# Regrouping the five far head pairs of a dilated attention layer: 2, 2, 1 in place of 1, 2, 2

## The chip, the core and the metric

The kernel runs on one core of a Trainium2 chip. The metric is the device time of one execution in microseconds (us). The core has five engines that are used here: TensorE (PE in the profile, with its weight loads as PEld), VectorE (DVE), ScalarE (ACT), GpSimd (POOL) and SyncE (SP, which here only starts transfers). They run side by side and wait for each other through semaphores. Each works through its own list of instructions in the order in which they stand there.

## The reference

A decoder trunk of two residual layers over 512 tokens of width 1024, all float32. The first layer mixes tokens by causal pooling, the second by attention; each is followed by a SwiGLU of inner width 2816, and one norm ends it. What matters here is the attention of the second layer. Its 16 heads of width 64 form three groups: heads 0 to 5 look at near keys (window 128, dilation 1), heads 6 to 10 at keys 4 apart, heads 11 to 15 at keys 16 apart.

```python
def attn_mixer(h, w_qkv, w_out):
    qkv = jnp.einsum('bsd,de->bse', h, w_qkv).reshape(B, S, 3, N_HEADS, HEAD_DIM)
    q = rope(qkv[:, :, 0]) * HEAD_DIM ** -0.5
    k = rope(qkv[:, :, 1])
    v = qkv[:, :, 2]
    for (window, dilation), n_g in zip(((128, 1), (512, 4), (2048, 16)), (6, 5, 5)):
        o_g, lse_g = dilated_window_attention(q[:, :, sl], k[:, :, sl], v[:, :, sl], window, dilation)
        outs.append(o_g)
        lses.append(logsumexp(lse_g, axis=-1) - math.log(n_g))
    alpha = softmax(stack(lses, axis=-1), axis=-1)
    merged = concatenate([o_g * 3 * alpha[:, :, g] for g, o_g in enumerate(outs)], axis=2)
    return merged @ w_out
```

Inside `dilated_window_attention` each query has a masked softmax over its keys (maximum, exponential, sum), the weights multiply the values, and the log of the sum plus the maximum goes into `lse`.

## The kernel before, in words

**Products.** Each float32 product is made of three matmuls: an operand is split into a rounded high part and a rest, and high x high, high x low and low x high are added up in PSUM. So each weight tile that a DMA brings (`wraw`) goes through a cast on ACT (`whi`, line 139) and a subtraction on DVE (`wlo`, line 143). Five such tiles are held; as `weights` is called for one step, the casts of tiles for later steps are issued, and a cast can start when PE is through with the tile whose place it takes.

**Steps.** The attention is a list of numbered steps. Steps 0 to 15 are the projections of q and k for the eight head pairs t = 0 to 7 (step 2t is q of pair t, 2t + 1 is k; `project`, lines 227 to 229, 24 matmuls). After each, `rope` turns the result: DVE shuffles and multiplies (859, 860), POOL multiplies the shuffled copy (861), DVE adds (865). Steps 16 to 18 project the values of the six near heads (m = 0, 1, 2). ACT copies each result out of PSUM (`ropea`, 1115 before, 1114 after); when the next projection is issued, `turn` transposes it with four PE transposes (1106 before, 1105 after), and ACT copies them into `v` (1107, then 1106). Steps 19 to 26 project the values of the far heads, in two halves of four steps, each step with six matmuls into each of four PSUM banks (1129 to 1131, then 1128 to 1130); the results are copied out after steps 22 and 26 by ACT (1137) and DVE (1135).

**Scores.** `later(step)`, called at the end of every step, does what is due: first transposes, then at most one visit with scores. A visit falls due three steps after its last k. The near pairs t = 0, 1, 2 have a visit each (`near_scores`). The far pairs t = 3 to 7 go through `far_scores`, which takes one pair or two: PE makes eight small matmuls per pair (925; the trace shows each as two), DVE scales and masks each head into `e` (935), takes the maxima (938, 879), and ACT makes four exponentials per head (`soften`, 881). Two steps later PE transposes the first pair's weights (955, four per far head), three steps later the second's; ACT or DVE copies them into `pT` (960, 958).

**PSUM.** There are eight banks: four named `mm`, two named `sc` (pool `psc`) and two named `tp` (pool `ptr`). Each name is a ring, and a tile can be written when the last reader of the tile that had the bank is done. A visit's first pair takes the two `sc` banks, a second pair takes two `mm` banks. `turn` takes a `tp` bank for m = 0 and an `sc` bank for m = 1 and 2.

**Group weights.** After step 19 `group_sums` (1027 to 1037) combines maxima and sums over the heads: one exponential on ACT (1029), a few small DVE operations and four small DMAs. After step 21 `group_weights` (1042 to 1069) makes the groups' shares with a second exchange by DMA (1062, waited for in 1069), and after step 23 one PE transpose (1077) spreads them.

**What sets the order.** PE's instructions stand in the order of the code. The other engines' lists are ordered by a planner when the kernel is built, by dependencies and priorities, so that an edit in the code can move their instructions in ways that it does not spell out.

Of the kernel before, what the change touches and what calls it, by code (L numbers as in the profile page):

```python
# [10 lines left out]
F32 = mybir.dt.float32  # L11
# [6 lines left out]
P = 128  # L18
# [40 lines left out]
def trunk_kernel(ctx: ExitStack, tc: tile.TileContext, x_in, xT, gam, gains, consts, ident_d, w0, wT, w1, wv, w_down, out):  # L59
# [171 lines left out]
    def project(j, hi, lo):  # L231
        ps = mm.tile([P, S], F32, name="mm")
        whi, wlo = weights(j)
        for k in range(NC):
            mm3(ps, whi[:, k, :], wlo[:, k, :], hi[:, k, :], lo[:, k, :], k == 0, k == NC - 1)
        return ps
# [26 lines left out]
    class Norm:  # L263
# [49 lines left out]
        def turn(self, b, half, tp):  # L313

            for j in range(4):
                at = half * S + j * P
                nc.tensor.transpose(tp[:, j, :], self.tile(b)[:, at : at + P], ident)
# [78 lines left out]
    with ExitStack() as pctx:  # L396
# [26 lines left out]
        for c in range(NC):  # L423
# [13 lines left out]
            k = 0 if c < 2 else c % 2  # L437
# [393 lines left out]
    with ExitStack() as actx:  # L831
# [4 lines left out]
        psc = actx.enter_context(tc.tile_pool(name="psc", bufs=2, space=bass.MemoryType.PSUM))  # L836
        ptr = actx.enter_context(tc.tile_pool(name="ptr", bufs=2, space=bass.MemoryType.PSUM))
# [18 lines left out]
        def rope(ps, t, name):  # L856
            a = aw.tile([P, S], F32, name="ropea")
            sw = aw.tile([P, S], F32, name="ropeb")
            nc.vector.stream_shuffle(sw, ps, PARTNER)
            nc.vector.tensor_mul(a, ps, cosr)  # L860
            nc.gpsimd.tensor_mul(sw, sw, sinr)
            out = aw.tile([P, S], F32, name=name, bufs=3)

            if t >= 3:
                nc.vector.tensor_add(out, a, sw)
            elif name == "k":
                nc.vector.tensor_add(out.rearrange("p (b r i) -> p b r i", b=4, r=R), blocks_of(a), blocks_of(sw))
            else:
                by_r = lambda z: z.rearrange("p (r j) -> p r j", r=R)
                nc.vector.tensor_add(out.rearrange("p (j r) -> p r j", r=R), by_r(a), by_r(sw))  # L870
            return out
# [90 lines left out]
        pend_sc, pend_tr = [], []  # L962

        def later(step):


            while pend_tr and pend_tr[0][0] <= step:
                _, h, e = pend_tr.pop(0)
                transposes(h, e)
                if HEAD_GROUP[h] == 0:  # L970
                    break
            if pend_sc and pend_sc[0][0] <= step:
                _, run, args = pend_sc.pop(0)

                pend_tr.extend((step + 2 + n // 2, *got) for n, got in enumerate(run(*args)))
# [25 lines left out]
        for t in range(8):  # L1001
            pq = pqk[2 * t] if t < 2 else project(j_qk[2 * t], h_hi, h_lo)
            q = rope(pq, t, "q")
            later(2 * t)
            pk = pqk[1] if t == 0 else project(j_qk[2 * t + 1], h_hi, h_lo)
            k = rope(pk, t, "k")
            later(2 * t + 1)
            if t in (4, 6):
                first = (t, q, k)
            elif t in (5, 7):  # L1010
                pend_sc.append((2 * t + 3, far_scores, (first, (t, q, k))))
            else:
                pend_sc.append((2 * t + 3, far_scores, ((t, q, k),)) if t == 3 else (2 * t + 3, near_scores, (t, q, k)))

        ring = [ap.tile([P, S], F32, name=f"LB{g}") for g in range(3)]
        sums = ap.tile([P, 2, 3, 4], F32, name="gsums")
# [83 lines left out]

        def turn():
            m, vt = to_turn.pop(0)

            tp = ptr.tile([P, 4, P], F32, name="tp") if m == 0 else psc.tile([P, 4, P], F32, name="sc")
            for b in range(4):
                nc.tensor.transpose(tp[:, b, :], vt[:, b * P : (b + 1) * P], ident)
            nc.scalar.copy(v[:, :, m * P : (m + 1) * P], tp)

        step = 16
        for m in range(3):  # L1110
            ps = project(j_v0[m], h_hi, h_lo)
            if to_turn:
                turn()
            vt = aw.tile([P, S], F32, name="ropea")
            nc.scalar.copy(vt.rearrange("p (b r i) -> p b r i", b=4, r=R), blocks_of(ps))
            to_turn.append((m, vt))
            between(step)
            step += 1
        for part in range(2):
            at = VA + part * VB  # L1120
            pv = [mm.tile([P, S], F32, name="mm") for _ in range(4)]
            for c in range(4):
                whi, wlo = weights(j_v[part][c])
                for b in range(4):
                    for kk in range(2):
                        kc = 2 * c + kk
                        o = pv[b][:, :VB]
                        xh, xl = (z[:, kc, b * P : (b + 1) * P] for z in (h_hi, h_lo))
                        nc.tensor.matmul(o, lhsT=xh, rhs=whi[:, kk, :], start=kc == 0, stop=False)  # L1129
                        nc.tensor.matmul(o, lhsT=xh, rhs=wlo[:, kk, :], start=False, stop=False)  # L1130
                        nc.tensor.matmul(o, lhsT=xl, rhs=whi[:, kk, :], start=False, stop=kc == NC - 1)
                    if c == 3:
                        with tc.high_priority(URGENT):
                            if b // 2:
                                nc.vector.tensor_copy(v[:, b, at : at + VB], pv[b][:, :VB])
                            else:
                                nc.scalar.copy(v[:, b, at : at + VB], pv[b][:, :VB])
                if to_turn:
                    turn()
                between(step)  # L1140
                step += 1
# [105 lines left out]
```

## Time and profile before

| | |
|---|---|
| median of three runs | 1001.42 us (1000.78 to 1001.96) |
| the profiled execution | 1000.55 us |
| its span, first to last instruction | 998.8 us |
| TensorE clock granted | 0.999 of full speed |
| PE busy | 990.8 us (99%) |
| DVE busy | 784.4 us (79%) |
| ACT busy | 529.1 us (53%) |
| POOL busy | 113.1 us (11%) |
| steps 8 to 26 of the attention | about 506 to 603 us of the span |

All times inside the span are from one profiled execution; what lies outside the span (1000.55 - 998.8, about 1.8 us) is the start and the end of the launch. Rows of the timeline give the start, the duration and the engine of an instruction. Matmuls overlap, so the distance between two starts on PE tells what one costs, and the duration doesn't. Rows of the chain of waits give the start of a piece, its length, and its engine, and are read downwards in time.

### The profile page before, as it was taken

The page shows a single profiled execution, that of the slowest core. Times are in us where ns is not written, and L with a number is a line of the kernel's source. Part 1 is how long each engine was busy: PE and PEld are TensorE (multiplying, and loading weights), DVE is VectorE, ACT ScalarE, POOL GpSimd, SP SyncE. Part 2 cuts the span into 40 slices and gives each one's busy share as a digit, 9 for nine tenths or more (in the row PEclk, how much of TensorE's full clock was granted, in tenths as well). Part 3 has the DMA queues.
Part 4 walks back from the last instruction along what each step waited for, and adds up shares of the span by engine and source line. Part 5 has one row for each costly group of instructions (what it writes and reads, how often), then busy time and mean ns, then how long its engine had stood idle before and what let it go on. Part 6 is the DMA issues. An engine that isn't in the chain of part 4 may idle for free.

```text
span 998.8 us, 16590 instructions
## 1 busy us (share of the span) xinstructions
PE 990.8 (99%) x6575; PEld 908.1 (91%) x6575; DVE 784.4 (79%) x1116; ACT 529.1 (53%) x838; POOL 113.1 (11%) x114
## 2 busy tenths in 40 slices
PE   9999999999999999999999999999999999999997
PEld 8888999989989998989888899899998998999896
DVE  6475899898888888777887457479989889788875
ACT  5573666545644554573543544356654554455354
POOL 0002010110111100002112023101011101211000
PEclk9999999999999999999999999999999999999999
DMA  9457276668559755524211249527666855975522
GB/s 335 177 168 190 63 197 174 152 189 234 149 128 290 179 137 155 182 71 134 85 56 53 83 141 267 103 61 191 179 159 198 235 148 121 294 176 141 153 66 84
DMA packets 76461, 157.29 MB, mean 157 GB/s; under 512 B 5904, under 2 KB 6288, under 8 KB 76384
## 3 DMA queue, kind: packets, MB, share of 16 engines
q1 hardware_dynamic: 58000, 121.00, 36.2%
q0 software_dynamic: 18096, 34.98, 20.5%
q8 instruction: 51, 0.84, 0.3%
q10 hardware_dynamic: 288, 0.27, 0.1%
q14 instruction: 26, 0.21, 0.1%
HBM read 154.08 MB, written 2.13 MB: 156 GB/s over the span
## 4 chain that ended last, share of the span: by engine, by line
PE 98%; ACT 1%; DVE 0%; issue 0%; ACTq 0%
PE p L625 25%; PE r L625 13%; PE r L712 10%; PE mm L625 6%; PE p L712 5%; PE mm L766 4%; PE mm L227 4%; PE mm L229 4%; PE mm L228 4%; PE mm L712 2%; PE early L443 2%; PE mm L363 2%; PE mm L361 2%; PE mm L362 2%; PE mm L1129 1%; PE tp L955 1%
## 5 line engine op out<-in xcount | busy, mean ns | idle before, releaser
L139 ACT CAST whi<-wraw 128x1024 fp32r<-128x1024 f32 (+2 forms) x189 | 184.8, 981 | 184.3 <-issue 50.8
L143 DVE TENSOR_TENSOR wlo<-wraw,whi 128x1024 fp32r<-128x1024 f32 (+2 forms) x190 | 221.1, 1165 | 74.8 <-ACT whi L139 74.1
L139 ACT CAST whi<-vraw 128x1024 fp32r<-128x1024 f32 (+1 forms) x102 | 99.6, 976 | 144.8 <-DVE vraw L145 53.7
L625 PE MATMUL p<-t_hi,wlo 128*128 128x256 f32 x528 | 149.8, 284 | 0.0
L625 PE MATMUL p<-t_lo,whi 128*128 128x256 f32 x528 | 149.4, 283 | 0.0
L625 PE MATMUL p<-t_hi,whi 128*128 128x256 f32 x528 | 148.4, 281 | 0.0
L143 DVE TENSOR_TENSOR wlo<-vraw,whi 128x1024 fp32r<-128x1024 f32 (+1 forms) x102 | 114.9, 1127 | 13.9 <-ACT whi L139 13.7
L625 PEld LDWEIGHTS p<-t_hi,whi 128*128 128x128 f32 x528 | 100.0, 189 | 0.0
L625 PE MATMUL r<-h_hi,wlo 128*128 128x256 f32 x352 | 99.9, 284 | 0.0
L625 PEld LDWEIGHTS p<-t_hi,wlo 128*128 128x128 f32 x528 | 99.6, 189 | 0.0
L625 PE MATMUL r<-h_lo,whi 128*128 128x256 f32 x352 | 99.6, 283 | 0.0
L625 PEld LDWEIGHTS p<-t_lo,whi 128*128 128x128 f32 x528 | 99.3, 188 | 0.0
L625 PE MATMUL r<-h_hi,whi 128*128 128x256 f32 x352 | 99.0, 281 | 0.0
L145 DVE TENSOR_TENSOR vraw<-vraw,wraw 128x1024 f32<-128x1024 f32 x68 | 76.6, 1127 | 0.8
L107 POOL DMA_DIRECT2D wraw<-w x22 | 26.6, 1211 | 436.1 <-DVE wlo L143 126.2
L625 PEld LDWEIGHTS r<-h_hi,whi 128*128 128x128 f32 x352 | 66.7, 189 | 0.0
L625 PEld LDWEIGHTS r<-h_hi,wlo 128*128 128x128 f32 x352 | 66.4, 189 | 0.0
L625 PEld LDWEIGHTS r<-h_lo,whi 128*128 128x128 f32 x352 | 66.2, 188 | 0.0
L227 PE MATMUL mm<-h_hi,whi 128*128 128x512 f32 (+1 forms) x176 | 64.9, 369 | 0.0
L229 PE MATMUL mm<-h_hi,wlo 128*128 128x512 f32 (+1 forms) x176 | 63.6, 361 | 0.0
L228 PE MATMUL mm<-h_lo,whi 128*128 128x512 f32 (+1 forms) x176 | 63.4, 360 | 0.0
L712 PE MATMUL r<-whi,u_lo 128*128 128x512 f32 x144 | 56.1, 390 | 0.0
(329 smaller groups left out, 2493.2 us busy)
## 6 DMA issues: line engine op xcount, KB each, us to landing
wraw<-w SPq DMA_DIRECT2D x116, 512.0 KB, 4.9
wraw<-w_down SPq DMA_DIRECT2D x32, 512.0 KB, 3.6
vraw<-w SPq DMA_DIRECT2D x22, 512.0 KB, 5.5
wraw<-w POOLq DMA_DIRECT2D x22, 512.0 KB, 7.6
vraw<-w POOLq DMA_DIRECT2D x22, 512.0 KB, 9.0
wraw<-wT SPq DMA_DIRECT2D x16, 512.0 KB, 4.4
wraw<-w_down SPq DMA_DIRECT2D x24, 256.0 KB, 2.6
vraw<-w_down SPq DMA_DIRECT2D x6, 512.0 KB, 5.4
```

The source lines that it names most:

```text
L107: nc.gpsimd.dma_start(dst, more, accum_op=ALU.add)
L139: nc.scalar.copy(hi[:, :n], raw[:, :n])
L143: nc.vector.tensor_sub(lo[:, :n], raw[:, :n], hi[:, :n].bitcast(F32))
L145: nc.vector.tensor_add(raws[into][:, :n], raws[into][:, :n], raws[more][:, :n])
L227: nc.tensor.matmul(ps, lhsT=whi, rhs=xhi, start=first, stop=False, **kw)
L228: nc.tensor.matmul(ps, lhsT=whi, rhs=xlo, start=False, stop=False, **kw)
L229: nc.tensor.matmul(ps, lhsT=wlo, rhs=xhi, start=False, stop=last, **kw)
L361: nc.tensor.matmul(ps, lhsT=xhi, rhs=w[0][:, k, :], start=first, stop=False)
L362: nc.tensor.matmul(ps, lhsT=xhi, rhs=w[1][:, k, :], start=False, stop=False)
L625: nc.tensor.matmul(ps[:, g, :], lhsT=w[:, g, c, :], rhs=xx[:, c, :], start=i in (0, 1, 3) and g + c + k == 0, stop=c == 3 and k == 2, skip ...
L712: nc.tensor.matmul(acc[t], lhsT=u, rhs=w, start=i in (0, 1, 3) and c + k == 0, stop=c == len(pairs) - 1 and k == 2, skip_group_check=True,)
L766: nc.tensor.matmul(ps, lhsT=u, rhs=w[:, m, :], start=z + m + k == 0, stop=z == 1 and m == 1 and k == 2,)
```

## The change

Two edits, both in how the work is grouped; no product is added or left out.

```diff
-            if t in (4, 6):
+            if t in (3, 5):
                 first = (t, q, k)
-            elif t in (5, 7):
+            elif t in (4, 6):
                 pend_sc.append((2 * t + 3, far_scores, (first, (t, q, k))))
             else:
-                pend_sc.append((2 * t + 3, far_scores, ((t, q, k),)) if t == 3 else (2 * t + 3, near_scores, (t, q, k)))
+                pend_sc.append((2 * t + 3, far_scores, ((t, q, k),)) if t == 7 else (2 * t + 3, near_scores, (t, q, k)))
...
         def turn():
             m, vt = to_turn.pop(0)
-
-            tp = ptr.tile([P, 4, P], F32, name="tp") if m == 0 else psc.tile([P, 4, P], F32, name="sc")
+            tp = psc.tile([P, 4, P], F32, name="sc")
```

The visits with far scores were at the ends of steps 9 (pair 3), 13 (pairs 4, 5) and 17 (pairs 6, 7). They are now at the ends of steps 11 (pairs 3, 4), 15 (pairs 5, 6) and 17 (pair 7). The far transposes, eight for a pair, were at steps 11, 15, 16, 19 and 20; they are now at 13, 14, 17, 18 and 19. All three turns now take an `sc` bank, so the `sc` ring is shared between the turn at step 17 and the scores that follow at once. From line 1103 on the lines stand one lower.

The first place is PE's list at the end of step 17, behind the projection of m = 1. `sc` is a bank of that ring, `tp` one of the other, `ropea` the copied values of m = 0, `e` the exponentials of a far head. The names in brackets are the engines whose semaphores an instruction waits for. Before:

```order
L1106 MATMUL tp<-ident,ropea 128x128 [waits Activation_49]
L1106 MATMUL tp<-ident,ropea 128x128 x3
L925 MATMUL sc<-k,q 128x128 x8
L925 MATMUL mm<-k,q 128x128 [waits DVE_49]
L925 MATMUL mm<-k,q 128x128 x7
```

The same place now:

```order
L1105 MATMUL sc<-ident,ropea 128x128 [waits DVE_49,Activation_49]
L1105 MATMUL sc<-ident,ropea 128x128 x3
L955 MATMUL tp<-ident,e 128x128 x4
L955 MATMUL tp<-ident,e 128x128 [waits DVE_49]
L955 MATMUL tp<-ident,e 128x128 x3
L925 MATMUL sc<-k,q 128x128 [waits PE_49]
L925 MATMUL sc<-k,q 128x128 [waits Activation_49]
L925 MATMUL sc<-k,q 128x128 x6
```

Eight transposes now stand between the turn and the scores, one pair of scores is gone from the visit, and the second matmul of the scores waits for ACT: it writes the `sc` bank that ACT copies the turn out of.

The second place is ACT's list from the first values (m = 0) to the exponential of the group sums. Before, with the 16 exponentials of pairs 6 and 7 in the middle, here as their first and their last rows:

```order
L139 CAST whi<-wraw 128x640 [waits DMAHW5_49,PE_49,Activation_49]
L1115 COPY ropea<-mm 128x512 [waits DVE_49,PE_49]
L960 COPY pT<-tp 128x512 [waits PE_49]
L139 CAST whi<-wraw 128x640 [waits DMAHW6_49,PE_49,Activation_49]
L1115 COPY ropea<-mm 128x512 [waits DVE_49,PE_49]
L1107 COPY v<-tp 128x4x128 [waits PE_49]
L881 ACTIVATE e,den<-e,neg 128x128 [waits DVE_49]
L881 ACTIVATE e,den<-e,neg 128x128 x3
```

and now, from the last exponentials of pairs 5 and 6, which are the visit of step 15:

```order
L881 ACTIVATE e,den<-e,neg 128x128 x3
L1114 COPY ropea<-mm 128x512 [waits PE_49]
L139 CAST whi<-wraw 128x640 [waits DMAHW5_49,Activation_49]
L139 CAST whi<-wraw 128x640 [waits DMAHW6_49,PE_49,Activation_49]
L1114 COPY ropea<-mm 128x512 [waits PE_49]
L1106 COPY v<-sc 128x4x128 [waits PE_49]
L960 COPY pT<-tp 128x512 [waits PE_49]
L881 ACTIVATE e,den<-e,neg 128x128 [waits DVE_49]
```

The copy of the values of m = 0 now stands behind 16 exponentials, and two casts stand between it and the copies of m = 1 and of the turn; behind them are 8 exponentials in place of 16.

The third place is DVE's list at the end of step 15, where the visit of pairs 5 and 6 has come in:

```order
L859 STREAM_SHUFFLE ropeb<-mm 128x512 [waits PE_49]
L860 TENSOR_TENSOR ropea<-mm,angles 128x512
L143 TENSOR_TENSOR wlo<-wraw,whi 128x640 [waits DMAHW4_49,Activation_49]
L865 TENSOR_TENSOR k<-ropea,ropeb 128x512 [waits DVE_49,Pool_49]
L935 SCALAR_TENSOR_TENSOR e<-sc,gain 128x512 [waits PE_49] x2
L938 TENSOR_REDUCE mx<-e 128x4 [waits DVE_49] x2
L879 TENSOR_SCALAR neg<-mx 128x4 [waits DVE_49]
```

The scores' first DVE operation (935) stands behind the whole rope of k of pair 7 and one weight subtraction, as it stood at step 13 before behind the rope of pair 6 and a subtraction of 1024 columns.

## The prediction, before the changed kernel had run

> **What bounds the kernel now.** I read the page first, then PE's waits, then the chain of waits through the attention, then the timelines of PE, DVE and ACT around its weak places.
>
> ```profile
> span 998.8 us, 16590 instructions
> PE 990.8 (99%) x6575; PEld 908.1 (91%) x6575; DVE 784.4 (79%) x1116; ACT 529.1 (53%) x838; POOL 113.1 (11%) x114
> PE mm L261 <- DVE odd_rows L255: 1.1, 1, 1.1
> PE mm L1129 <- ACT ropea L1115: 0.3, 1, 0.3
> ```
>
> The first two rows are the page's, the other two are all of PE's waits. PE is the bound: 990.8 of 998.8 us, and it waits twice in the whole program, once at the start, which the change doesn't touch, and once for 0.3 us at step 19, for the copy of the values of m = 2. So there is little to win, and a loss needs a wait on PE that is not there now. The question is one of tenths of a microsecond: which small stalls go, and which come. The chain of waits shows what is behind the one at step 19:
>
> ```profile
> 567.70 4.78 ACT e L881 x25
> 572.64 1.34 ACT e L881 x7
> 573.98 0.47 ACT v L1107
> 574.45 0.49 ACT ropea L1115
> 574.99 0.41 PE mm L1129
> ```
>
> The visit of step 17 has four heads. Their 16 exponentials (with the reads of their sums) hold ACT from 567.70 to 573.98, and behind them stand two copies; the second frees the last `mm` bank that step 19 needs. PE's timeline shows what that costs:
>
> ```profile
> 574.42 0.31 PE L1131 MATMUL mm<-whi,h_lo 128*128 128x320 f32 x1
> 574.99 0.41 PE L1129 MATMUL mm<-whi,h_hi 128*128 128x320 f32 x1 [0.26 <-ACT ropea L1115]
> 575.24 0.31 PE L1130 MATMUL mm<-wlo,h_hi 128*128 128x320 f32 x1
> ```
>
> and a second, smaller stall of the same kind four steps later, which the list of waits doesn't name:
>
> ```profile
> 590.18 0.31 PE L1130 MATMUL mm<-wlo,h_hi 128*128 128x320 f32 x1
> 590.33 0.31 PE L1131 MATMUL mm<-whi,h_lo 128*128 128x320 f32 x1
> 590.65 0.42 PE L1129 MATMUL mm<-whi,h_hi 128*128 128x320 f32 x1
> 590.90 0.31 PE L1130 MATMUL mm<-wlo,h_hi 128*128 128x320 f32 x1
> ```
>
> These matmuls follow each other at 0.15 (590.18 to 590.33). From 574.42 to 575.24 are 0.82 where 0.30 would do: the stall costs 0.52, more than the 0.26 that the wait shows, since a matmul's record outlasts the start of the next by 0.16, and the first after a gap takes 0.1 more. From 590.33 to 590.90 are 0.57 where 0.30 would do: 0.27. The cause of the second is on DVE:
>
> ```profile
> 589.26 0.18 DVE L1069 TENSOR_TENSOR den<-den,mx 128x24 f32<-128x24 f32 x1 [3.41 <-DMA mx<-gw]
> 589.37 0.83 DVE L143 TENSOR_TENSOR wlo<-wraw,whi 128x640 fp32r<-128x640 f32 x1
> 590.11 0.88 DVE L1135 COPY v<-mm 128x320 f32<-128x320 f32 x2
> ```
>
> DVE's list stands still for 3.41 us for the second exchange of the group weights, and the copy that frees the bank (1135) comes only behind it; the first of the two ends at about 590.6.
>
> **The change part by part.** *The new wait: the turn and the scores in one ring.* At the end of step 17 PE turns m = 0 into one `sc` bank, makes eight transposes, and its second score matmul needs that bank back, once ACT has copied it. The pieces are in the trace, though not in this order:
>
> ```profile
> 563.40 0.60 PE L1106 MATMUL tp<-ident,ropea 128*128 128x128 f32 x4
> 563.92 1.16 PE L925 MATMUL sc<-k,q 64*128 64x128 f32 x16
> ...
> 576.41 1.04 PE L955 MATMUL tp<-ident,e 128*128 128x128 f32 x8
> 577.20 0.39 PE L1129 MATMUL mm<-whi,h_hi 128*128 128x320 f32 x1
> 577.43 0.31 PE L1130 MATMUL mm<-wlo,h_hi 128*128 128x320 f32 x1
> ```
>
> These are PE's. On ACT, at the same end of step 17:
>
> ```profile
> 563.41 0.73 ACT L139 CAST whi<-wraw 128x640 fp32r<-128x640 f32 x1 [4.65 <-issue]
> 564.04 0.58 ACT L1115 COPY ropea<-mm 128x512 f32<-128x512 f32 x1
> 564.52 0.59 ACT L1107 COPY v<-tp 128x512 f32<-128x512 f32 x1
> ```
>
> Call T the start of the turn (563.40 here). PE needs 0.52 for the turn, 0.79 for the transposes and about 0.13 for the first score matmul: it wants the bank at T + 1.44. ACT makes the cast that the end of step 17 released, at T, then the copy of m = 1, then the copy of the turn, which ends at 565.11, T + 1.71, and reaches PE 0.05 later (574.94 to 574.99 in the chain above). So even if ACT is free at T, PE waits 0.32: the lower end of this cost. Queued behind that matmul are the rest of the scores and the whole of step 18, so a wait there is paid in full.
>
> *Is ACT free at T?* In the list of the change, ACT has 16 exponentials of the visit of step 15, the copy of m = 0 and a first cast ahead of the cast at T. Where these end is read from the visit of step 13 before, which had the same neighbours: a rope on DVE and POOL ahead of it, two projections behind it.
>
> ```profile
> 537.70 1.16 PE L925 MATMUL sc<-k,q 64*128 64x128 f32 x16
> 550.70 1.03 PE L955 MATMUL tp<-ident,e 128*128 128x128 f32 x8
> ...
> 523.06 1.22 DVE L143 TENSOR_TENSOR wlo<-wraw,whi 128x1024 fp32r<-128x1024 f32 x1
> 539.04 2.01 DVE L143 TENSOR_TENSOR wlo<-wraw,whi 128x1024 fp32r<-128x1024 f32 x1
> 540.97 0.68 DVE L865 TENSOR_TENSOR k<-ropea,ropeb 128x512 f32<-128x512 f32 x1
> 551.08 0.82 DVE L143 TENSOR_TENSOR wlo<-wraw,whi 128x640 fp32r<-128x640 f32 x1 [1.30 <-ACT whi L139]
> ...
> 538.70 1.27 POOL L861 TENSOR_TENSOR ropeb<-ropeb,angles 128x512 f32<-128x512 f32 x1 [4.13 <-DVE ropeb L859]
> 550.33 1.34 ACT L139 CAST whi<-wraw 128x640 fp32r<-128x640 f32 x2
> ```
>
> With S the start of the scores, the two projections end at S + 13.00, which will be T; ACT turns from the last exponential to a cast at 550.33, S + 12.63. Taken over unchanged, the copy of m = 0 (0.58) would reach PE at S + 13.26 and hold up the turn itself by 0.26: the upper end. But at step 15 the subtraction ahead of the scores has 640 columns, not 1024. The 1024 columns took 2.01 beside POOL's multiply of the rope and 1.22 alone, 640 alone 0.82. If the neighbour adds the same 0.79 to 640 columns, that is 1.61, an estimate, 0.40 less than at step 13.
>
> Then ACT is through with the exponentials at S + 12.23, T - 0.77; the copy of m = 0 is seen at T - 0.14, just in time for the turn. The next in the list starts 0.48 after a copy (564.04 to 564.52) and 0.63 after a cast: the first cast lasts to T + 0.34, the second to T + 0.97, the copy of m = 1 to T + 1.45, and the copy of the turn is seen at T + 2.09. PE wants T + 1.44: **+0.65**, my value, between 0.32 (ACT free at T) and 1.05 (step 13's time unchanged: 0.26 at the turn, then the copy of the turn at T + 2.49 against a want of T + 1.70).
>
> The Trainium skill ("SBUF — State Buffer", section "SBUF: two separate sides") says that DVE and GpSimd share a pair of ports under an exclusive lock: a DVE operation with two SBUF inputs and a GpSimd operation that reads SBUF exclude each other for the whole instruction. The 2.01 agrees: begun at 539.04, with POOL busy to 539.97. By that rule the 640 columns would run only behind POOL's multiply, the wait would be 0.81 and the change worth 0.07; it speaks against a visit that is moved behind such a rope.
>
> *The copy of m = 2.* The last visit has 8 exponentials in place of 16, at 0.39 each, 3.1 us fewer on ACT ahead of the copy that PE waited for. It then follows the end of step 18 at once, and step 19 needs the bank only 18 matmuls later. That stall goes whole: **-0.52**.
>
> *The group weights.* The exponential that starts them, line 1029, stood behind those copies too:
>
> ```profile
> 574.83 0.26 ACT L1029 ACTIVATE mx<-mx 128x64 f32<-128x64 f32 x1
> ```
>
> That is T + 11.43. After the change it stands behind the copies of m = 2, of a turn and of a head's transposes. PE is through with the scores at about T + 3.1 (0.52 + 0.79 + 0.65 + 1.16), with step 18 5.5 later (half of 13.00 less two pairs of scores), with a turn and four transposes at T + 9.5, and the last copy takes it to T + 10.1: 1.3 us earlier. From 1029 to 589.26 everything follows it (DVE and two exchanges by DMA), so the copy that ended at 590.6 ends near 589.3, ahead of 590.5, when PE wants the bank: **-0.27**.
>
> *What the visits themselves cost PE* is the same, five pairs of scores and 40 transposes. One return to the stream falls away, since two groups of transposes now stand beside a turn; a return costs 0.08 (577.20 to 577.43 are 0.23 in place of 0.15): **-0.08**, and at least nothing.
>
> *The visit at step 11* repeats step 13's surroundings two steps earlier. Its exponentials hold ACT for 6 us, and casts wait behind them; the same visit at step 13 made two casts run together at 550.33, and PE lost nothing by it, because tiles are cast some five steps of 5.5 us ahead. I cost it at nothing; without that cover it would be up to those 6 us.
>
> *The sum:* 0.65 - 0.52 - 0.27 - 0.08 = -0.22, on the profiled execution's 1000.55. The median of the runs is 0.87 above that execution, and I carry the difference over: 1001.42 - 0.22 = **1001.2 us**.
>
> **The rivals.**
>
> *ACT is in time at step 17.* The cost is 0.32: -0.55, **1000.9**. For it: POOL and the subtraction must meet to delay each other, and 640 columns are soon through. Against: the list has them in step 13's order.
>
> *POOL holds the subtraction up whole,* as in the row of 539.04: the cost is 0.81, -0.06, **1001.4**.
>
> *The copy of m = 0 is late, and the turn with it.* This is the side of slower. Its place is the end of step 17; it decides as soon as the exponentials of step 15 end after S + 12.37, and from there each tenth is a tenth of PE, since nothing stands between the turn and the stream. With step 13's row unchanged, and no gain from a return, it is 1.05 - 0.52 - 0.27 = +0.26, **1001.7**. For it: the row itself. Against: the shorter subtraction. To be slower by 2 us it would need exponentials 1.8 us later still, and no row has such a delay in this place.
>
> *The second stall stays,* because the exchange starts no earlier: 0.27 comes back, +0.05, **1001.5**. Against it are the 1.3 us, of which a fifth would do.
>
> *A weight tile comes too late behind the visits of steps 11 or 15:* up to the 6 us above, so **1003 to 1007**; the row of 550.33 speaks against it.
>
> **How the numbers follow.** My forecast has 0.40, ACT in time 0.20, POOL's hold 0.13, the late turn 0.12, the second stall 0.10, the late tile 0.03, and 0.02 is left for what I don't see. A measurement of this kernel can tell a change from none at about 0.2%, 2.0 us; all but the last two cases lie within 0.6 us of the time before, so the chances are 0.04 faster, 0.92 the same, 0.04 slower. The terms alone span 1000.9 to 1001.7. The three runs of before span 1.2 us, and the median of new runs can be off by half of that on either side, so I take 1000.1 to 1002.3.
>
> **What would show it.** In PE's waits the row on the copy of m = 2 is gone, and a new one stands at the scores (925) for the copy of the turn, with a stall of 0.3 to 0.9 us in the timeline. No stall at about 590. ACT through with the exponentials of step 15 some 12.2 us after their scores began, with 640 columns of subtraction beside POOL at 1.6. Line 1029 at T + 10.1. It would be wrong if PE waits at the turn itself by more than 0.3, if a wait for `whi` or `wlo` shows on PE, or if the stream outside steps 9 to 26 takes another time than before.

## The result, and the profile after

The changed kernel took 1002.56 us, median of 22 runs (1000.59 to 1003.55); the kernel before, run beside it, 1000.87 us, median of 22 (1000.12 to 1002.04). The ratio is 1.0013, with a 95% interval of 1.0007 to 1.0018: slower by about 1.3 us, with the medians 1.7 apart. That is inside the 0.2% that the prediction named as its limit, but the sign is against the -0.22 us, and the median lies above the range of 1000.1 to 1002.3. The runs also spread further (3.0 us against 1.9). The profiled execution took 1001.83 us against 1000.55.

The first two rows are the page's for the changed kernel, the others all of PE's waits in it:

```profile
span 1000.1 us, 16584 instructions
PE 991.9 (99%) x6575; PEld 909.2 (91%) x6575; DVE 784.8 (78%) x1116; ACT 529.8 (53%) x838; POOL 113.1 (11%) x114
PE mm L261 <- DVE odd_rows L255: 1.1, 1, 1.1
PE early L443 <- ACT h_hi L418: 0.3, 1, 0.3
PE sc L925 <- ACT v L1106: 0.2, 1, 0.2
```

The wait at step 19 (`mm <- ropea`) is gone, and the one foreseen at the scores (925) is there. (The one on line 443 is in the program's first 30 us; the kernel before run again has it too, with 1.0.) What happened around it is in PE's and ACT's timelines of the changed kernel:

```profile
563.47 0.60 PE L1105 MATMUL sc<-ident,ropea 128*128 128x128 f32 x4
...
565.53 1.16 PE L925 MATMUL sc<-k,q 64*128 64x128 f32 x14 [0.17 <-ACT v L1106]
566.61 0.50 PE L227 MATMUL mm<-h_hi,whi 128*128 128x512 f32 x1
```

```profile
562.70 0.56 ACT L1114 COPY ropea<-mm 128x512 f32<-128x512 f32 x1
...
564.89 0.58 ACT L1106 COPY v<-sc 128x512 f32<-128x512 f32 x1
573.90 0.28 ACT L1029 ACTIVATE mx<-mx 128x64 f32<-128x64 f32 x1
```

With T = 563.47, PE is back in the stream at T + 3.14 (predicted 3.12, with 0.65 of waiting in it). ACT ends the copy of the turn at T + 2.00 (predicted 2.04, seen at 2.09), and the group weights begin at T + 10.43 (predicted 10.1). The copy that PE wanted at about 590.5 now starts 1.5 us earlier on DVE, and the second stall is gone too (the first row ends the exchange, the last is the copy):

```profile
587.73 0.18 DVE L1069 TENSOR_TENSOR den<-den,mx 128x24 f32<-128x24 f32 x1 [4.07 <-DMA mx<-gw]
...
588.58 1.03 DVE L1134 COPY v<-mm 128x320 f32<-128x320 f32 x2
```

So the places that the prediction spoke of went much as it said. The time is lost 20 us later, in a stage that it did not look at: the merging loop, in which PE multiplies the softmax weights with the values, pair by pair (t = 0 to 7); DVE multiplies each result by the group weights of its heads (`LB`, `even_rows`), which also empties one of the four `mm` banks (lines 1167 and 1171 before, 1166 and 1170 after); and ACT and DVE split the product for the out-projection (320, 321). POOL has brought those weights out of `far` in DRAM by broadcasts of 128 KB (1086). Here are the last 77 matmuls of the loop and the first of the out-projection, of the kernel before and then of the changed one:

```profile
610.54 5.15 PE L1159 MATMUL mm<-pT,v 128*64 128x128 f32 x77
615.62 0.50 PE L361 MATMUL sc<-whi,h_hi 128*128 128x512 f32 x1
```

```profile
610.47 6.02 PE L1158 MATMUL mm<-pT,v 128*64 128x128 f32 x77
616.41 0.50 PE L361 MATMUL sc<-whi,h_hi 128*128 128x512 f32 x1
```

At their start the changed kernel is 0.07 ahead; at their end it is 0.79 behind: 5.94 from the one row to the other in place of 5.08, a loss of 0.86. On ACT and DVE the reason can be read, before and then after:

```profile
606.92 1.05 ACT L139 CAST whi<-wraw 128x1024 fp32r<-128x1024 f32 x1 [3.93 <-DVE o L1167]
...
608.00 1.23 DVE L143 TENSOR_TENSOR wlo<-wraw,whi 128x1024 fp32r<-128x1024 f32 x1 [1.12 <-ACT whi L139]
612.17 1.13 DVE L1171 TENSOR_TENSOR o<-mm,even_rows 128x512 f32<-128x512 f32 x1
```

```profile
608.76 1.04 ACT L139 CAST whi<-wraw 128x1024 fp32r<-128x1024 f32 x1 [4.56 <-DMA wraw<-w]
...
609.84 1.23 DVE L143 TENSOR_TENSOR wlo<-wraw,whi 128x1024 fp32r<-128x1024 f32 x1 [3.02 <-ACT whi L139]
613.73 1.12 DVE L1170 TENSOR_TENSOR o<-mm,even_rows 128x512 f32<-128x512 f32 x1
614.90 1.34 PEld L1158 LDWEIGHTS mm<-pT,v 128*64 128x64 f32 x16 [0.26 <-DVE o L1170]
```

The cast at the head of each is not the attention's. It splits the first weight tile of the feed-forward that follows, which nobody needs yet. But it stands in ACT's list ahead of the splits of the loop, and its subtraction (143) stands in DVE's list ahead of the products that empty PE's banks. In the changed kernel it waits for its DMA until 608.76. (In the kernel before, the row names the product 1167, which ended at 606.89, as what the cast waited for last; the tile had landed just ahead of it, at 606.83.) The product that frees the bank of t = 3, which t = 7 needs, then starts at 613.73 in place of 612.17 and ends at 614.85, and PE, out of banks, goes on with the last 16 matmuls at 614.90: the last row, of its weight loads. The tile was asked for at the same time in both kernels (598.72 and 598.65), as the next rows show, each list of transfers with the microseconds to landing at the end; before, then after:

```profile
wraw<-w SPq DMA_DIRECT2D x1, 512.0 KB, 8.1
597.83 2.59 POOL L1086 DMA_DIRECT2D LB<-far  x5 [3.02 <-DMA far<-ropea]
```

```profile
wraw<-w SPq DMA_DIRECT2D x1, 512.0 KB, 10.0
596.26 3.11 POOL L1086 DMA_DIRECT2D LB<-far  x6 [1.53 <-DMA far<-ropea]
```

The broadcasts began 1.57 us earlier, five in place of two ahead of the tile's load, and the load took 10.0 us instead of 8.1. They began earlier because the write of the far weights landed in 1.8 us instead of 3.3.

The other 0.51 us of the 1.30 between the two spans lie behind 616 us: from the start of the out-projection to the end of the span are 383.69 us here and 383.18 before. It is not the kernel's: the same distance is 383.04 to 383.24 in 12 of the 14 traces of this study, that of the changed kernel run again among them (383.23), and 383.65 in one other. In these two executions PE works more slowly from about 700 us on: by the starts of its rows, 24 matmuls of the feed-forward (line 625) take 2.88 us there, from 707 to 744, and 2.85 in the kernel before and in the changed kernel run again. Why stays open: the granted clock is the same in these stretches (1.00), and no wait stands there.

### The profile page after: what moved, and what is told of

It reads as the page before. It is cut to its first block, busy times and chain, and to the rows that moved or that the text cites. A ratio compares the mean times of both kernels' runs of the same rounds, so it can differ in the third digit from the quotient of the medians.

```text
span 1000.1 us, 16584 instructions
## 1 busy us (share of the span) xinstructions
PE 991.9 (99%) x6575; PEld 909.2 (91%) x6575; DVE 784.8 (78%) x1116; ACT 529.8 (53%) x838; POOL 113.1 (11%) x114
## 4 chain that ended last, share of the span: by engine, by line
PE 98%; ACT 1%; DMA 0%; DVE 0%; SPq 0%; issue 0%; ACTq 0%
PE p L625 25%; PE r L625 13%; PE r L712 10%; PE mm L625 6%; PE p L712 5%; PE mm L227 4%; PE mm L766 4%; PE mm L229 4%; PE mm L228 4%; PE mm L712 2%; PE mm L361 2%; PE mm L363 2%; PE mm L362 2%; PE early L443 2%; PE mm L1128 1%; PE mm L1130 1%
```

## The experiments

**Theory A**: the weight tile lands late because of the earlier broadcasts, and its cast holds the loop. **Theory B**: a draw of one execution. **Theory C**: the new wait at the scores costs more than its row shows. Four kernels went first, on one chip, with 33 runs of the kernel before beside them (1000.80 us median).

### Both kernels again

> The kernel before once more, unchanged, for a second trace. Theory A (the 0.9 us are lost in the far heads' values because the first weight tile of the layer's feed-forward lands later, and its cast on ACT and its subtraction on DVE stand in front of the splits of the attention's output): here the tile lands before 607.5 us, its cast starts before 607.7, and the out-projection starts near 615.6; time 1000.5 to 1001.3. Theory B (the lost time is the draw of one execution, not of the kernel): this second trace may show the late tile as well, with the out-projection near 616.4.

> The changed kernel once more, unchanged. Theory A: five broadcasts of far weights stand ahead of the tile's load again, it lands after 608.2 us, the cast of it holds the splits, the out-projection starts near 616.4; time 0.8 to 1.8 us above the kernel before. Theory B: this trace may show the tile early and the out-projection near 615.6, and the time is within 0.6 us of the kernel before. Theory C (the new wait of the scores for the copy of the turn at 565 us is the loss, and larger than the 0.5 us seen): the values start later than 610.7 us in this trace.

The kernel before took 1000.88 (ratio 1.0001, 0.9992 to 1.001), the changed kernel 1002.00 (1000.51 to 1003.17; ratio 1.0011, 1.0003 to 1.002). The profiled execution of the changed kernel was one of its quick ones, 1000.54, and it shows why:

```profile
607.88 1.05 ACT L139 CAST whi<-wraw 128x1024 fp32r<-128x1024 f32 x1 [3.82 <-DMA wraw<-w]
610.37 5.27 PE L1158 MATMUL mm<-pT,v 128*64 128x128 f32 x77
```

The broadcasts began at 596.15, early as in the first trace, but the load took 9.2 us in place of 10.0, the cast started 0.88 sooner, and the loop lost 0.12 in place of 0.86. I had expected the tile after 608.2 in any execution of the changed kernel; it comes late by different amounts, and that is the spread of its times. Theory B falls on the medians, which repeat. Theory C falls too: the 77 matmuls begin at 610.37, no later than before.

### The cast put behind the splits

```diff
-                nc.scalar.copy(hi[:, :n], raw[:, :n])
+                with tc.issue_after(item["cast_behind"]) if "cast_behind" in item else nullcontext():
+                    nc.scalar.copy(hi[:, :n], raw[:, :n])
...
+            if t == 3:
+                queue[j_wo[-1] + 1]["cast_behind"] = first.ins
```

(`first` is the ACT instruction of the split of pair t; the subtraction follows its cast.)

> The changed kernel with one edit: the cast of that weight tile on ACT (and with it its subtraction on DVE) is put behind the split of the fourth far pair's output; its load stays where it is. Theory A: the tile lands late still (after 608.2), but the splits no longer stand behind its cast; the 0.9 us come back, out-projection near 615.5, time 0.7 to 1.1 us below the changed kernel. If the cast only moves the delay to the feed-forward's first matmuls, the time stays and a wait for the tile shows there. Theory B and theory C: time as the changed kernel within 0.4 us.

It took 1000.67 (1000.23 to 1001.06; ratio 0.9999, 0.999 to 1.0008), 1.3 below the changed kernel beside it, a little more than expected.

```profile
613.31 1.04 ACT L140 CAST whi<-wraw 128x1024 fp32r<-128x1024 f32 x1
610.38 5.15 PE L1160 MATMUL mm<-pT,v 128*64 128x128 f32 x77
```

Here the load took 10.1 us, landed at 608.65 as in the changed kernel's first trace, and cost nothing. So it is not the late tile itself that costs, but what stands behind its cast in two lists. No wait for the tile shows up in the feed-forward.

### The broadcasts held back

```diff
-            nc.gpsimd.dma_start(far, rows[: 4 * H, :])
+            sent = nc.gpsimd.dma_start(far, rows[: 4 * H, :])
+            with tc.issue_after(sent.ins):
+                for _ in range(5):
+                    nc.gpsimd.memset(ring[0], 0.0)
```

> The changed kernel with one edit: four to five idle fills of 128x1024 on POOL behind the write of the far weights, some 1 to 1.5 us or more, so that the broadcasts start as late as in the kernel before or later (597.8 us). Theory A: two or fewer broadcasts stand ahead of the tile's load, it lands before 607.5, the cast does not hold the splits, and the time is 0.5 to 1.1 us below the changed kernel, unless the fills hold the broadcasts so long (past about 600 us) that the far values wait for their weights, which would show as DVE waiting for the broadcasts at L1169 or so. Theory B and theory C: as the changed kernel within 0.4 us.

It took 1000.27 (1000.15 to 1000.85; ratio 0.9995, 0.9986 to 1.0004), 1.7 below the changed kernel beside it, where 0.5 to 1.1 were expected. The fills are of 128x512, not 128x1024.

```profile
596.71 0.54 POOL L1089 DMA_DIRECT2D LB<-far  x1
...
597.71 2.58 POOL L1089 DMA_DIRECT2D LB<-far  x5
606.36 1.05 ACT L139 CAST whi<-wraw 128x1024 fp32r<-128x1024 f32 x1 [3.18 <-DMA wraw<-w]
610.17 5.15 PE L1161 MATMUL mm<-pT,v 128*64 128x128 f32 x77
```

The first broadcast was held less than expected (596.71), the rest to 597.71, so three stood ahead of the tile's load in place of five. The load took 7.9 us again, and the loss is gone with the cast in its old place: the second half of theory A.

### The same late tile in the kernel before, and a control

```diff
+        if "decoy" in item:
+            with tc.issue_after(raws["last"].ins):
+                nc.sync.dma_start(item["decoy"], item["src"][0])
-        nc.sync.dma_start(dst, item["src"][0])
+        raws["last"] = nc.sync.dma_start(dst, item["src"][0])
```

(set for the first tile of the feed-forward alone; `decoy` is a tile in DRAM.)

> The kernel before, with its pairs grouped as they were, and one transfer more: 512 KB of the same weights are copied to memory that nobody reads, issued on SP right ahead of the load of the first feed-forward weight tile; nothing is left out. Theory A: the tile lands 1 to 3 us later than in the kernel before (after 608.2), the block of 77 value matmuls lengthens by what it lands after about 607.6, and the time rises by as much, 0.6 to 2.5 us. Rival (the late tile matters only together with the regrouped pairs): the time stays within 0.4 us though the tile lands late.

> The kernel before with the same edit as the changed kernel had: the cast of the first feed-forward weight tile is put behind the split of the fourth far pair. Theory A: in the kernel before the tile lands early enough (607.4 and 606.8 us in its two traces), so the edit gives nothing: within 0.3 us of the kernel before; the block of 77 value matmuls stays at 5.15 us. What is then left between this and the changed kernel with the same edit (1000.67) is the balance of the terms of the prediction, put there at -0.22 us. Rival (the edit itself gains something, whatever the tile does): 0.5 us or more below the kernel before.

With 512 KB more ahead of the tile, the kernel before took 1002.57 (1000.74 to 1003.51; ratio 1.0015, 1.0006 to 1.0024): the changed kernel's median and spread without its change. The load took 11.0 us, and in PE's rows the loop now breaks up (... stands for 48 matmuls, in two pieces):

```profile
610.63 1.05 ACT L142 CAST whi<-wraw 128x1024 fp32r<-128x1024 f32 x1 [5.96 <-DMA wraw<-w]
611.34 2.19 PE L1163 MATMUL mm<-pT,v 128*64 128x128 f32 x29
...
618.66 0.50 PE L364 MATMUL sc<-whi,h_hi 128*128 128x512 f32 x1
```

From 611.34 to 618.66 are 7.32 in place of 5.08. The control, with its cast behind the splits and no decoy, took 1000.55 (ratio 0.9998, 0.9989 to 1.0007), as the kernel before beside it (1000.83, 30 runs).

### Why the broadcasts start early: a miss and a hit

The first try delayed the exchange of the group weights, by a copy and three fills on POOL ahead of its transfers:

```diff
+            held = nc.gpsimd.tensor_copy(ring[0][:, :12], share.rearrange("p g b -> p (g b)"))
+            for _ in range(3):
+                with tc.issue_after(held.ins):
+                    held = nc.gpsimd.memset(ring[0], 0.0)
             for b in range(4):
-                nc.gpsimd.dma_start(back[:, b : b + 1], share[32 * b : 32 * b + 32, 0, :])
+                with tc.issue_after(held.ins):
+                    nc.gpsimd.dma_start(back[:, b : b + 1], share[32 * b : 32 * b + 32, 0, :])
```

> The changed kernel with the group weights put back to about the time that they had before: a small copy and three fills of 128x512 on POOL (0.54 us each) ahead of the four transfers that bring the group weights to their queries, so that the last product with them on DVE comes at 589.2 to 589.8 instead of 587.7. Theory A's start of the chain (the earlier weights let the weight loads on SP go earlier, the far weights' write then lands in 1.8 us instead of 3.0 to 3.3, and the broadcasts stand ahead of the tile's load): here the write takes 3 us again, the broadcasts start after 597.5, the tile lands before 607.6, the block of 77 takes 5.15 us, the stall near 590 for the copy on DVE may come back (0.3 to 0.5 us), and the time is 0.4 to 0.9 us below the changed kernel. Rival (the broadcasts start early for another reason): the write still lands in 1.8 us, and the time is the changed kernel's.

It took 1001.54 (1000.31 to 1002.28; ratio 1.0009, 1.0 to 1.0017), and the loop lost 1.06. It says little, since the edit did not do what it was for. The transfers went out 1.76 later, at 584.09, but the product with them came only 0.23 later, and the subtraction that follows started at 590.21, as in the changed kernel (590.24):

```profile
587.96 0.18 DVE L1074 TENSOR_TENSOR den<-den,mx 128x24 f32<-128x24 f32 x1 [0.77 <-DMA mx<-gw]
590.21 1.23 DVE L143 TENSOR_TENSOR wlo<-wraw,whi 128x1024 fp32r<-128x1024 f32 x1 [0.64 <-ACT whi L139]
```

In the kernel before, that subtraction starts at 590.91, when DVE is through with the copy (1135). It frees the buffer of the weight load that SP issues next, at 592.15 before and 591.49 after, and it is behind this load that the far weights' write is sent. So the second try delayed the subtraction alone:

```diff
-                                nc.vector.tensor_copy(v[:, b, at : at + VB], pv[b][:, :VB])
+                                copied = nc.vector.tensor_copy(v[:, b, at : at + VB], pv[b][:, :VB])
+                                if (part, b) == (0, 3):
+                                    with tc.issue_after(copied.ins):
+                                        for _ in range(3):
+                                            held = nc.vector.memset(ring[1], 0.0)
+                                    queue[j_wo[0]]["behind"] = held.ins
```

> The changed kernel with three fills of 128x512 on DVE behind the second copy of the value accumulators near 589.5 us, ahead of the subtraction of the next weight tile, which then starts at about 591 in place of 590.24 (590.91 in the kernel before). Theory A, sharpened: the load that takes the buffer freed by this subtraction is issued at about 592.2 in place of 591.4, the far weights' write lands behind it and takes about 3 us again in place of 1.8, the broadcasts start after 597.5, fewer of them stand ahead of the tile's load, and the block of 77 value matmuls is back at 5.15 to 5.3 us: 0.4 to 1.2 us below the changed kernel in time. Rival (the write lands fast for another reason, the earlier group weights or fewer transfers): the write takes 1.8 us still and the time is the changed kernel's.

It took 1000.81 (1000.21 to 1001.26; ratio 0.9999, 0.999 to 1.0008; the kernel before beside it 1000.92, 33 runs).

```profile
591.09 1.16 DVE L143 TENSOR_TENSOR wlo<-wraw,whi 128x1024 fp32r<-128x1024 f32 x1
592.28 3.95 SPq L105 DMA_DIRECT2D wraw<-wT  x3
596.38 3.10 POOL L1086 DMA_DIRECT2D LB<-far  x6 [1.94 <-DMA far<-ropea]
606.79 1.04 ACT L139 CAST whi<-wraw 128x1024 fp32r<-128x1024 f32 x1 [4.16 <-DMA wraw<-w]
610.18 5.15 PE L1163 MATMUL mm<-pT,v 128*64 128x128 f32 x77
```

With the subtraction 0.85 later the loss is gone, so when it runs matters. But two numbers on the way missed: the write took 2.2 us, not 3, and the broadcasts began at 596.38, not after 597.5, with four ahead of the load. And still the load took 8.3 us. So the way from the subtraction to the late tile is shown only in part: the write took 1.8 in all eight traces with the regrouped pairs and no fills on DVE, and 2.8 to 3.6 in all five of the kernel before and its variants, but that the start of the broadcasts alone decides is not shown. The queues tell more. These are the transfers from 598 to 606 us, packets, megabytes and share of the 16 engines, q1 with SP's loads, q0 with POOL's: of the kernel before, the changed kernel and this one.

```profile
q1 hardware_dynamic: 717, 1.39, 56.3%
q0 software_dynamic: 233, 0.65, 31.9%
```

```profile
q1 hardware_dynamic: 524, 1.02, 49.3%
q0 software_dynamic: 319, 0.90, 46.9%
```

```profile
q1 hardware_dynamic: 626, 1.22, 50.7%
q0 software_dynamic: 368, 1.03, 47.0%
```

Where the tile is late, SP's queue moves 1.02 to 1.13 MB; where it isn't, 1.22 or more (1.30 with the fills on POOL; the kernel before with 512 KB ahead of the tile, late for that reason, is apart at 1.64). The Trainium skill ("DMA: Bandwidth & Descriptors", section "Queues, rings and completion order") says that each DMA engine goes round the queues that have work, a packet at a time; a load therefore slows down as soon as another queue is filled, and not only when something stands ahead of it. The first two kernels agree: 0.65 MB of broadcasts become 0.90, and the loads lose 0.37. The third does not: it moved the most broadcasts of all (1.03) and more through both queues (2.25 MB against 1.92), and its tile was in time. The number of broadcasts issued ahead of the tile's load sorts the traces better: with five the load took 9.2 to 11.4 us, with one to four 6.7 to 8.3, in all but the trace with 512 KB ahead. Why four and five differ stays open.

| kernel | first broadcast ahead of the tile's load, us | the load took, us | cast starts, us | lost in the loop, us |
|---|---|---|---|---|
| before, two traces | 0.89, 1.18 | 8.1, 7.9 | 606.92, 607.46 | 0, 0 |
| changed, two traces | 2.39, 2.40 | 10.0, 9.2 | 608.76, 607.88 | 0.86, 0.12 |
| exchange delayed (the miss) | 2.16 | 10.2 | 608.93 | 1.06 |
| turn in the other ring (below) | 2.40 | 11.4 | 610.62 | 2.28 |
| subtraction delayed | 1.98 | 8.3 | 606.79 | 0 |
| fills on POOL | 1.64 | 7.9 | 606.36 | 0 |
| before, with 512 KB ahead | 1.38 | 11.0 | 610.63 | 2.24 |

Lost is the time from the first of the 77 matmuls to the out-projection, less 5.08. From a start of the cast at about 607.8 on, each microsecond that it comes later costs about 0.8. The cast moved behind the splits, above, has no line here: its load took 10.1 with 2.39 ahead, and nothing was lost.

### The turn in its old ring

```diff
-            tp = psc.tile([P, 4, P], F32, name="sc")
+            tp = ptr.tile([P, 4, P], F32, name="tp") if m == 0 else psc.tile([P, 4, P], F32, name="sc")
```

> The changed kernel with one part undone: the first value chunk's turn goes back to the ring of two banks that the transposes of the weights use, so that the scores of step 17 no longer wait for its copy on ACT. The prediction put that wait at 0.65 us; in the trace of the changed kernel PE lost about 0.5 there. If the ring is what costs it, the 0.5 us come back and the transposes of the next pair wait instead for at most as much: -0.5 to +0.2 us against the changed kernel in the stretch from 560 to 575 us. The late weight tile is not touched by it, so theory A has the block of 77 above 5.15 us here, and the time at 0.5 below to 0.3 above the changed kernel.

It took 1003.24 (1002.28 to 1003.52; ratio 1.0023, 1.0013 to 1.0033), worse than expected.

```profile
563.34 0.60 PE L1105 MATMUL tp<-ident,ropea 128*128 128x128 f32 x4
565.40 0.66 PE L955 MATMUL tp<-ident,e 128*128 128x128 f32 x4 [1.03 <-ACT v L1106]
567.08 0.50 PE L227 MATMUL mm<-h_hi,whi 128*128 128x512 f32 x1
```

PE is back at T + 3.74 in place of T + 3.14: now the pair's transposes wait for the copy, and they want the bank earlier than the scores did. So with the pairs grouped this way the `sc` ring is the better place by 0.60, and this does not remove the new wait. The tile was late too (11.4 us, 2.28 lost).

### What is left of the prediction's sum

The last three kernels ask for the sum without the accident: the fills once more, both cures together, and the fills in the kernel before (with which the control of the cast, above, belongs).

> The kernel before with the five fills on POOL behind the far weights' write, as the changed kernel had them (1000.27). A control for what the fills do by themselves: in the kernel before the broadcasts start after the tile's load is nearly issued anyway, so theory A expects 1000.5 to 1000.9, the tile no earlier than 606.3 and the block of 77 at 5.15 us. Rival (the fills gain by themselves): 1000.3 or less.

> The changed kernel with the five fills on POOL once more, for its distance to the kernel before: 1000.27 the first time. Expected 1000.1 to 1000.6, and 0.2 to 0.6 us below the same fills in the kernel before; if the distance is nothing, the terms that the prediction put at -0.22 us are not there.

> The changed kernel with both edits, the fills and the cast behind the fourth split. Theory A: with the broadcasts held the tile lands in time already, so the second edit adds nothing: 1000.1 to 1000.6, as the fills alone. If it is lower by 0.3 us or more, the cast still cost something in the fills' kernel.

Beside a kernel before of 1000.92 (33 runs), the fills alone took 1000.58 (1000.05 to 1001.15; ratio 0.9996, 0.9987 to 1.0005), fills and cast 1000.60 (0.9997, 0.9988 to 1.0006), the fills in the kernel before 1000.92 (0.9999, 0.999 to 1.0007). The last has a miss in it: its cast came at 606.88, as it should, yet the loop took 5.73 instead of 5.08, since there the fills made the far weights themselves late:

```profile
DVE o L1170 <- DMA LB<-far: 4.1, 1, 4.1
```

PE's own rows measure the sum better than the times. From the first matmul of the q and k projections (at 464.87 us before) to the first of the 77 are 145.67 us in the first trace of the kernel before, 146.07 in the second, and 145.60, 146.06 and 146.09 in its variants; in eight traces with the regrouped pairs they are 145.51 to 145.56, and in the ninth, with the turn in the other ring, 146.12. So up to the loop the change gains about 0.1 against two of the five traces of the kernel before and its variants, and about 0.5 against the other three, in which the stall at 590 is larger. This is the second trace of the kernel before:

```profile
590.68 0.31 PE L1131 MATMUL mm<-whi,h_lo 128*128 128x320 f32 x1
591.38 0.41 PE L1129 MATMUL mm<-whi,h_hi 128*128 128x320 f32 x1 [0.39 <-DVE v L1135]
591.63 0.31 PE L1130 MATMUL mm<-wlo,h_hi 128*128 128x320 f32 x1
```

From 590.68 to 591.63 are 0.95 where 0.30 would do: 0.65, against 0.27 in the trace on which the prediction rested. The best version here is thus the changed kernel with the fills on POOL: 1000.27 and 1000.58 in its two rounds against 1000.80 and 1000.92. Its medians are below those of both kernels, but its intervals against the kernel before hold 1; what is shown is that it undoes the loss.

## Why the prediction was wrong

**Right, by the runs:** PE's return after the new wait at the scores (T + 3.14 against 3.12; the stall itself is nearer 0.53 than 0.65, since the scores begin at 564.87 and stop until 565.53 behind two matmuls put at 0.13, and the matmuls around it took 0.14 more than put), the stall of step 19 gone, no stall at 590, line 1029 at T + 10.43 against 10.1, the exponentials of step 15 through in time for the turn, no wait for a weight tile at the visits of steps 11 and 15. Of the sum of -0.22, -0.12 is measured up to the loop against the trace that it was made from, and about -0.5 against the other kind.

The estimate of the subtraction behind the first of these met the row, on DVE in the changed kernel:

```profile
551.80 1.61 DVE L143 TENSOR_TENSOR wlo<-wraw,whi 128x640 fp32r<-128x640 f32 x1
```

It was 1.61 for the 640 columns beside POOL's multiply. POOL's record runs from 551.45 to 552.73; if the subtraction had run only behind it, as the Trainium skill ("SBUF — State Buffer", section "SBUF: two separate sides") has it, it would have ended at 553.55, 1.75 us after its start. The row is 0.14 shorter, and so is the row at 539.04 on which the prediction rested (end at 541.05, against 539.97 + 1.22 = 541.19). Both began some 0.34 us into POOL's multiply, so the two rows don't decide between that rule and the prediction's 0.79; the wait of 0.81 that the prediction gave for the rule did not come (by its own sum, 1.75 in place of 1.61 would be a wait of 0.79).

**The step that failed** is *The group weights*: "From 1029 to 589.26 everything follows it (DVE and two exchanges by DMA), so the copy that ended at 590.6 ends near 589.3", **-0.27**. All of that happened (the copy starts at 588.58), and the term is right for what it looks at. It ends at the copy, and the sum puts everything behind the copy at nothing, without a reason, the merging loop included. There the runs show 0.86 lost in the first trace, 0.12 in the second, and 1.7 and 1.2 between the medians of the two rounds. The term does not ask what DVE, free earlier, does next: the subtraction that follows starts at 590.24 in place of 590.91, the next load goes out at 591.49 in place of 592.15, the far weights' write lands in 1.8 in place of 3.3 us, the broadcasts come down on the engines together with the feed-forward's first tile, and the cast of that tile stands ahead of the loop's splits. So the step that was booked as a gain of 0.27 most likely carried the loss with it. The end of this chain is shown: with the cast moved, or the broadcasts held, the loss goes, and a late tile alone brings it into the kernel before. Its beginning is shown by the fills on DVE as far as that a later subtraction takes the loss away; the links between, from the subtraction over the write to the early broadcasts, are read from the traces and argued.

**The sentence that would have caught it** is among the signs in which the prediction would be wrong: "if the stream outside steps 9 to 26 takes another time than before". It was named as a sign and not costed as a rival. The rival on a late weight tile had the right thing in mind, 1003 to 1007, but in another place (the visits' exponentials ahead of the casts) and for another reason; it does not describe what happened. The row to cost it from was in the trace of before: the cast at 606.92 stood in the list in front of the splits, with its DMA landed at 606.83, 0.1 us earlier. By the table it could come some 0.9 us later before it cost anything, and nothing in the prediction asked for that.

**The range** rested on three runs of the kernel before, which span 1.2 us. It took their spread over to the changed kernel, whose times span 3.0; with the cast moved or the broadcasts held they span 0.7 to 1.1, so the spread comes with the wait on the tile. The median of the three, 1001.42, was also 0.55 above that of the 22 runs beside the changed kernel (1000.87); from there the same sum gives 1000.65, and the measured time is 1.9 above it.

## What to carry to other kernels

When a change makes a chain end earlier, follow it one step past the engine that you care about: the buffer freed early, the load that goes out early, and the transfer that this load or its neighbours will meet. In an engine's list look for instructions of a later stage that wait for a DMA and stand ahead of urgent work; find out how much later such a cast or copy can start before the urgent work behind it is late (here some 0.9 us), since beyond that every change of the traffic ahead of it is a change of the time. Putting it behind the urgent work cost nothing here (1000.67, and 1000.55 in the kernel before). A kernel whose times spread wider after an edit may have gained a wait on a transfer: here 3.0 us in place of 1.9.

## What the runs showed of the hardware

Three fills of 0.5 us on DVE took away 1.2 us, median against median of the changed kernel run in another call. A load of 512 KB took 3.5 us when issued at 588.68 in the changed kernel. The feed-forward's first tile, as large and issued at 598.3 to 599.5, took 6.7 to 11.4 us; from 602 to 608 us the profile gives the 16 DMA engines as busy for 0.99 of their time before and 1.06 after, by the sum of their packets' times. In identical programs it took 10.0 and 9.2. A write of 32 KB took 1.8 us when the 512 KB load ahead of it had been issued 2.7 us before, 2.2 us at 1.6 and 3.3 us at 2.1 us before, so its time does not follow that distance alone; in every trace it landed after that load, by 0.2 to 1.3 us. And delaying a set of four small transfers by 1.76 us made what waits for them only 0.23 later: the last of them took 2.06 us in place of 3.54, and landed behind a load of 512 KB in both kernels.
